# Grid attention in a mixer kernel: the order of scores, scaling, transposes and values of sixteen pairs

## Chip, cores and metric

The kernel runs on one core of one Trainium2 chip. The metric is the device time of one execution in microseconds. The engines are PE (matmuls and transposes; PEld is its weight load), ACT, DVE, POOL and SP, which issues the DMAs. Each works through its instructions in the order in which the program gives them.

## The reference

One layer of a hybrid backbone for 512 latent tokens and 256 context tokens of width 1024, all in float32. A normalised input goes through one wide projection. Its columns feed three mixers: a short gated convolution, a gated linear recurrence in both directions, and attention on the latent grid of 8 rows by 64 columns. The three are gated, merged and projected, and a mixture of 16 experts follows. The change concerns the attention:

```
s_loc = einsum(q, k of the window) * scale + bias     # 256 keys of the grid
s_ctx = einsum(q, k of the context) * scale           # 256 keys of the context
p     = softmax(concat(s_loc, s_ctx))                 # 512 scores a query
o     = einsum(p_loc, v) + einsum(p_ctx, v_ctx)
```

Each of 8 heads has 64 channels. The queries are taken in blocks of 16 columns by 8 rows, 128 queries to a block.

## The kernel before

**Pairs.** The attention is cut into 16 pairs n: two heads that lie together on the 128 partitions (`hp`, four of them) by one block of 128 queries (`cb`, four of them). Four functions make the work of a pair, and each issues at once all that it does on every engine.

- `att_scores(n)`, lines 883 to 902: four matmuls on PE write the scores of both heads into two banks of tag hg (two buffers). Then for each head u in turn: DVE adds the bias (line 897) and takes the row maximum (898), ACT computes the exponential and its row sum into a tile p (900).
- `att_scale(n)`, 904 to 910: for each head DVE takes the reciprocal of the sum (908) and multiplies p by it (909).
- `att_turn(n, u)`, 912 to 922: four PE transposes of p (917) into the bank tp, which has one buffer, and a copy by ACT into a tile pT (919).
- `att_values(n)`, 924 to 942: sixteen matmuls of the values with pT (934) into a bank of tag acc; after every fourth pair ACT and DVE (939, 940) split the result into a rounded and a remaining part.

**Foreground.** While this runs, PE also works through eight items of weights: two convolution gates with their products c, u (lines 953 to 968) and b (970 to 975), and two items of raw gates. An item has two blocks of eight steps; a step is three matmuls of 128x512 (line 453). After the eighth step of a block its result is evacuated by ACT (c, gate) or DVE (u, b). `use_item` (424 to 439) also hangs four pieces of the split of the next item's weights on steps 0, 2, 5 and 8: a cast on ACT (366) and a subtraction on DVE (367) that reads the cast. With three leftover steps that turn value rows (862 to 869) the foreground has 131 entries.

**Order.** The order of all instructions is the order of the Python calls. `weave` (180 to 192) lays the list `att_bg` evenly among the foreground entries: after each of these it issues as many entries of the list as are due by the share of the foreground's cost that is done. An entry None issues nothing but takes its place, so it sets distances. Before the change the list has 83 entries, five to a pair.

**Around it.** Before the stage lie the projections and the recurrence; behind it lie the remaining gates and the merge, and then the experts, whose weights are loaded into the tiles that the earlier stages give back.

Of the kernel before, what the change touches and what calls it, by code (L numbers as in the profile page):

```python
# [146 lines left out]
def mixer_moe(ctx: ExitStack, tc: tile.TileContext, a, out):  # L147
# [10 lines left out]
    def bank(tag):  # L158
        return psum.tile([128, 512], F32, tag=tag, name=tag, bufs=pbufs[tag])
# [8 lines left out]
    def g512(dt=F32):  # L168
        return gen.tile([128, 512], dt, tag="g", name="g", bufs=NA_)
# [707 lines left out]
    def att_load(hp):  # L877
        for t in range(3):
            b_ = gen.tile([128, 2, 256], F32, tag="bias", name="bias", bufs=4)
            SP.dma_start(out=b_, in_=a["bias"][2 * hp:2 * hp + 2, :, 256 * t:256 * t + 256].rearrange("u p k -> p u k"))  # L880
            ast["b", hp, t] = b_

    def att_scores(n):
        def f():
            hp, cb = au[n]
            if cb == 3 and hp < 3:
                att_load(hp + 1)
            rs = [slice(64 * u, 64 * u + 64) for u in range(2)]
            ps = [bank("hg") for _ in range(2)]
            qs = nq[hp][:, 128 * cb:128 * cb + 128]  # L890
            for c, keys in enumerate((nk[hp][:, 64 * KB0[cb]:64 * KB0[cb] + 256],
                                      nkc[hp // 2][:, 256 * (hp % 2):256 * (hp % 2) + 256])):
                for u in range(2):
                    PE.matmul(ps[u][:, 256 * c:256 * c + 256], qs[rs[u]], keys[rs[u]], start=True, stop=True)
            for u in range(2):
                st_ = gen.tile([128, 4], F32, tag="st", name="st", bufs=4)
                V.tensor_tensor(ps[u][:, 0:256], ps[u][:, 0:256], ast["b", hp, BTYPE[cb]][:, u], op=ALU.add)
                V.tensor_reduce(st_[:, 0:1], ps[u], axis=AX.X, op=ALU.max, negate=True)  # L898
                p = g512()
                S.activation(p, ps[u], AF.Exp, bias=st_[:, 0:1], accum_out=st_[:, 1:2])  # L900
                ast["p", n, u] = (p, st_)
        return f

    def att_scale(n):
        def f():
            for u in range(2):
                p, st_ = ast["p", n, u]
                V.reciprocal(st_[:, 2:3], st_[:, 1:2])
                V.tensor_scalar(p, p, st_[:, 2:3], None, op0=ALU.mult)
        return f  # L910

    def att_turn(n, u):
        def f():
            p, _ = ast["p", n, u]
            pt = bank("tp")
            for c in range(4):
                PE.transpose(pt[:, 128 * c:128 * c + 128], p[:, 128 * c:128 * c + 128], ident)
            pT = g512()
            S.copy(pT, pt)
            ast["t", n, u] = pT  # L920
            del ast["p", n, u]
        return f

    def att_values(n):
        def f():
            hp, cb = au[n]
            pT = [ast.pop(("t", n, u)) for u in range(2)]
            if cb == 0:
                ast["o"] = bank("acc")
            po = ast["o"]  # L930
            vs = (nv["lat"][:, KB0[cb]], nv["lat"][:, KB0[cb] + 2], nv["ctx"][:, 0], nv["ctx"][:, 1])
            for c in range(4):
                for u in range(2):
                    PE.matmul(po[64 * u:64 * u + 64, 128 * cb:128 * cb + 128],
                              vs[c][:, 128 * hp + 64 * u:128 * hp + 64 * u + 64],
                              pT[u][:, 128 * c:128 * c + 128], start=(c == 0), stop=(c == 3))
            if cb == 3:
                hi, lo = g512(F32R), g512(F32R)
                S.copy(nat_q(hi), perm_q(po))
                V.tensor_tensor(nat_q(lo), perm_q(po), nat_q(hi.bitcast(F32)), op=ALU.subtract)  # L940
                yv[2][hp] = (hi, lo)
        return f

    att_bg = [att_scores(0)]
    for n in range(16):
        att_bg += [att_values(n - 1) if n else None, att_scale(n), att_scores(n + 1) if n < 15 else None,
                   att_turn(n, 0), att_turn(n, 1)]
    att_bg += [None, att_values(15)]


    cst = {}
# [172 lines left out]
    for pr in range(2):  # L1124
        for i in (2 * pr, 2 * pr + 1):
            n = 16 + 3 * pr + (i % 2)
            fg += use_item(n, [proj(n, 0, ev_c(i)), proj(n, 1, ev_u(i))])
        n = 18 + 3 * pr
# [367 lines left out]
```

## Time and profile before

| | us |
|---|---|
| median of 3 runs | 1749.94 |
| lowest and highest run | 1746.86, 1750.92 |
| profiled execution, its own time | 1747.9 |
| its span in the profile | 1745.7 |
| PE busy | 1633.8 (94%) |
| DVE busy | 570.7 (33%) |
| ACT busy | 369.2 (21%) |

The profile is of one execution. The span lies between its first and last instruction. A busy PE is not a PE at its peak, because matmuls overlap; the granted clock says at which share of full speed the throttle let it run. The stage of the change lies from about 392 to 562 us.

### The profile page before, as it was taken

Reading aid. Unit: us, or ns where it says so; the run is one execution under the profiler, and the core shown is the slowest. Engines: PE = TensorE matmul, PEld = TensorE weight load, DVE = VectorE, ACT = ScalarE, POOL = GpSimd, SP = SyncE. Lnnn points to the kernel's source line nnn. Section 1 sums busy time; section 2 is a strip of 40 time slices with the busy share of each in tenths; the row PEclk is TensorE's granted clock in tenths of the full one; section 3 lists DMA queues with packets and bytes.
Section 4 is the critical chain, followed back from the end, with each engine's and each line's share of the span. In section 5 each row is a group of like instructions: output and inputs, shape, how many; then the busy total and the mean of one; then the engine's idle time right before and its main releaser. Section 6 shows DMA issues by size and latency. Waiting matters only on the chain.

```text
span 1745.7 us, 20467 instructions
## 1 busy us (share of the span) xinstructions
PE 1633.8 (94%) x8382; PEld 928.4 (53%) x8382; DVE 570.7 (33%) x1135; ACT 369.2 (21%) x759; POOL 79.9 (5%) x150
## 2 busy tenths in 40 slices
PE   4999999998989999999999999999998998989988
PEld 2767888775666888896343343343432432424322
DVE  2518776445654343334012111121121121201121
ACT  3514445333434232323000000000000100000000
POOL 0314330000000000000000000000000000000000
PEclk8999999999999999999999999999999999999999
DMA  8870111111111332356999999999999999999997
GB/s 342 268 256 25 49 49 73 49 67 67 67 61 43 109 137 102 144 221 240 411 426 427 426 426 427 426 427 426 427 426 427 427 426 427 426 426 427 427 426 293
DMA packets 80745, 487.77 MB, mean 279 GB/s; under 512 B 8972, under 2 KB 12556, under 8 KB 25740
## 3 DMA queue, kind: packets, MB, share of 16 engines
q1 hardware_dynamic: 80652, 486.47, 68.2%
q8 instruction: 66, 1.08, 0.2%
q14 instruction: 27, 0.22, 0.0%
HBM read 484.34 MB, written 2.10 MB: 279 GB/s over the span
## 4 chain that ended last, share of the span: by engine, by line
PE 62%; DMA 18%; DVE 8%; ACT 2%; issue 1%; ACTq 0%; SPq 0%; DVEq 0%
PE pj L1365 17%; PE pj L453 17%; PE acc L1390 7%; DMA B<-in_w_exp_dram 7%; DMA W<-in_w_exp_dram 6%; PE pj L1016 4%; PE hg L1419 4%; PE hg L1333 3%; PE pj L1197 2%; DMA C<-in_w_exp_dram 2%; DMA A<-in_w_exp_dram 2%; DVE st L898 1%; DVE acc L1422 1%; DMA D<-in_w_exp_dram 1%; PE hg L724 1%
## 5 line engine op out<-in xcount | busy, mean ns | idle before, releaser
L453 PE MATMUL pj<-A,W 128*128 128x512 f32 x1536 | 410.8, 406 | 2.9 <-ACT W L366 1.9
L453 PEld LDWEIGHTS pj<-A,W 128*128 128x128 f32 x1536 | 275.6, 190 | 73.1 <-issue 21.4
L367 DVE TENSOR_TENSOR W<-W 128x512 fp32r<-128x512 f32 (+1 forms) x184 | 122.0, 686 | 167.0 <-ACT W L366 166.7
L1372 DVE TENSOR_TENSOR s<-s,pj 128x512 f32<-128x512 f32 x32 | 22.0, 687 | 444.4 <-PE pj L1365 357.7
L1365 PE MATMUL pj<-W,xe 128*64 128x512 f32 x688 | 155.1, 598 | 4.1 <-DMA W<-in_w_exp_dram 4.1
L1370 ACT ACTIVATE s<-pj 128x512 f32<-128x512 f32 x32 | 19.1, 597 | 556.6 <-PE pj L1365 556.6
L1365 PE MATMUL pj<-A,xe 128*64 128x512 f32 x512 | 116.8, 600 | 3.7 <-DMA A<-in_w_exp_dram 3.7
L1419 PE MATMUL hg<-ye,oht 64*128 64x512 f32 x240 | 100.6, 685 | 16.6 <-DVE acc L1422 16.6
L1365 PEld LDWEIGHTS pj<-W,xe 128*64 128x64 f32 x688 | 47.9, 137 | 104.8 <-issue 91.3
L366 ACT CAST W<-W 128x512 fp32r<-128x512 f32 (+1 forms) x184 | 103.3, 600 | 0.0
L1365 PE MATMUL pj<-B,xe 128*64 128x512 f32 x432 | 98.2, 596 | 5.1 <-DMA B<-in_w_exp_dram 5.1
L1422 DVE TENSOR_TENSOR acc<-acc,hg 128x512 f32<-128x512 f32 x120 | 77.7, 685 | 37.3 <-PE hg L1419 37.3
L1365 PEld LDWEIGHTS pj<-A,xe 128*64 128x64 f32 x512 | 35.1, 138 | 78.3 <-issue 65.4
L1419 PEld LDWEIGHTS hg<-ye,oht 64*128 64x128 f32 x240 | 32.8, 194 | 81.8 <-DVE acc L1422 69.6
L1411 DVE TENSOR_TENSOR ye<-mod,acc 64x512 f32<-64x512 f32 x30 | 20.6, 686 | 170.0 <-PE acc L1390 169.5
L1390 PE MATMUL acc<-W,at 128*64 128x512 f32 x320 | 71.5, 595 | 1.3 <-DMA W<-in_w_exp_dram 1.3
L1365 PEld LDWEIGHTS pj<-B,xe 128*64 128x64 f32 x432 | 29.7, 137 | 67.9 <-issue 54.0
L1380 ACT COPY at<-tp 128x512 f32<-128x512 f32 x32 | 18.7, 586 | 216.6 <-PE tp L1378 216.1
L453 PEld LDWEIGHTS pj<-C,W 128*128 128x128 f32 x384 | 59.2, 190 | 9.2 <-ACT y L625 0.8
L453 PE MATMUL pj<-C,W 128*128 128x256 f32 x384 | 61.7, 283 | 0.0
L1365 PE MATMUL pj<-C,xe 128*64 128x512 f32 x256 | 59.1, 603 | 1.0 <-DMA C<-in_w_exp_dram 1.0
L1333 PEld LDWEIGHTS hg<-ot,xn 128*128 128x128 f32 x512 | 57.9, 192 | 2.7 <-issue 2.7
(287 smaller groups left out, 1813.0 us busy)
## 6 DMA issues: line engine op xcount, KB each, us to landing
W<-in_w_exp_dram SPq DMA_DIRECT2D x126, 1024.0 KB, 19.5
A<-in_w_exp_dram SPq DMA_DIRECT2D x88, 1024.0 KB, 19.6
B<-in_w_exp_dram SPq DMA_DIRECT2D x85, 1024.0 KB, 19.5
C<-in_w_exp_dram SPq DMA_DIRECT2D x42, 1024.0 KB, 19.6
D<-in_w_exp_dram SPq DMA_DIRECT2D x42, 1024.0 KB, 19.6
W<-in_w_in_dram SPq DMA_DIRECT2D x34, 1024.0 KB, 4.8
y<-in_w_mod_dram SPq DMA_DIRECT2D x32, 256.0 KB, 6.0
g<-in_w_mod_dram SPq DMA_DIRECT2D x32, 256.0 KB, 5.2
```

The lines of the kernel that those rows point to most:

```text
L366: S.copy(hi[:, sl], raws[n][:, sl])
L367: V.tensor_tensor(lo[:, sl], raws[n][:, sl], hi[:, sl].bitcast(F32), op=ALU.subtract)
L453: PE.matmul(dst, w[wi][:, k, 128 * b:128 * b + 128], src[xi][:, k], start=(k == 0 and p == 0), stop=(k == KT - 1 and p == 2))
L1016: PE.matmul(st["p"], wb[wi][:, 4 * br + k], yv[br][k][xi], start=(k == 0 and p == 0), stop=(k == 3 and p == 2))
L1197: PE.matmul(st["p"][:, 256 * u:256 * u + 256], mm[k][mi][:, ts], w[wi][:, k], start=(k == 0 and p == 0), stop=(k == KT - 1 and p == 2))
L1333: PE.matmul(px[:, 128 * k:128 * k + 128], xn[:, i, 128 * kk:128 * kk + 128], ot[:, 128 * i:128 * i + 128], start=(i == 0), stop=(i == 3))
L1365: PE.matmul(pg[64 * u:64 * u + 64], xp[:, kk, 64 * (e % 2):64 * (e % 2) + 64], wt[:, k, 512 * u:512 * u + 512], start=(kk == 0), stop=(kk ...
L1372: V.tensor_tensor(est["s", j], est["s", j], pg, op=ALU.mult)
L1390: PE.matmul(est["y"][64 * u:64 * u + 64], lhs, wt[:, k, 512 * u:512 * u + 512], start=(kk == 0), stop=(kk == 15))
L1411: V.tensor_tensor(ye[us], mod5[us, 512 * u:512 * u + 512], y[us], op=ALU.mult)
L1419: PE.matmul(pc, oht[64 * u:64 * u + 64, 128 * i:128 * i + 128], ye[64 * u:64 * u + 64], start=True, stop=True)
L1422: V.tensor_tensor(av, av, pc, op=ALU.add)
```

## The change

The scores of pair 0 come first as before. Then each pair n has its two turns with the values of pair n-1 between them, then the scores of pair n+1, two empty entries, and the scaling of pair n+1. The functions themselves are the same. The list grows to 115 entries, seven to a pair.

```diff
-    att_bg = [att_scores(0)]
+    att_bg = [att_scores(0), None, None, None, att_scale(0)]
     for n in range(16):
-        att_bg += [att_values(n - 1) if n else None, att_scale(n), att_scores(n + 1) if n < 15 else None,
-                   att_turn(n, 0), att_turn(n, 1)]
-    att_bg += [None, att_values(15)]
+        att_bg += [att_turn(n, 0), att_values(n - 1) if n else None, att_turn(n, 1)]
+        att_bg += [att_scores(n + 1), None, None, att_scale(n + 1)] if n < 15 else [None, att_values(15)]
```

## Rows read from the trace of the kernel before

**Rows 1.** Stages by windows; columns: us, PE, PEld, DVE, ACT, POOL, clock, DMA, GB/s.
```profile
392.00:562.00 170.00, 150.04 (x904) 108.00 (x903) 89.97 (x187) 67.71 (x145) 0.00 (x0) 0.98 0.18 61
562.00:780.00 218.00, 217.78 (x1123) 185.78 (x1121) 86.98 (x142) 67.84 (x142) 10.29 (x8) 1.00 0.37 138
780.00:1745.00 965.00, 908.28 (x4218) 350.87 (x4218) 181.27 (x344) 75.28 (x139) 0.18 (x1) 0.99 0.98 410
```

**Rows 2.** Groups by line and shape, 388 to 565 us: busy, mean ns, idle before.
```profile
L917 PE MATMUL tp<-ident,g 128*128 128x128 f32 x128 | 20.1, 279 | 17.8 <-ACT g L919 16.3 <-ACT nvc L869 1.5
```

**Rows 3.** Timeline, scores of pair 4: start, us, engine, line [idle before <-releaser].
```profile
431.22 1.14 PE L894 MATMUL hg<-g 64*128 64x256 f32 x8
...
432.28 1.66 PE L453 MATMUL pj<-A,W 128*128 128x512 f32 x6
432.38 0.43 DVE L897 TENSOR_TENSOR hg<-hg,bias 128x256 f32<-128x256 f32 x1 [2.00 <-PE hg L894]
...
433.77 0.60 PE L917 MATMUL tp<-ident,g 128*128 128x128 f32 x4
433.91 0.69 DVE L898 TENSOR_REDUCE st<-hg 128x1 f32<-128x512 f32 x1
...
434.70 0.69 ACT L900 ACTIVATE g<-hg,st 128x512 f32<-128x512 f32 x1 [0.28 <-DVE st L898]
435.28 0.19 ACT L900 ACTIVATION_READ_ACCUMULATOR g<-hg,st 128x1 f32 x1
435.38 0.57 ACT L919 COPY g<-tp 128x512 f32<-128x512 f32 x1
...
436.00 0.66 PE L917 MATMUL tp<-ident,g 128*128 128x128 f32 x4 [0.93 <-ACT g L919]
...
436.70 0.59 ACT L919 COPY g<-tp 128x512 f32<-128x512 f32 x1 [0.75 <-PE tp L917]
...
438.99 2.33 PE L453 MATMUL pj<-A,W 128*128 128x512 f32 x9
```

**Rows 4.** Timeline, an unbroken run of projection matmuls in the merge stage.
```profile
599.68 11.27 PE L453 MATMUL pj<-A,W 128*128 128x512 f32 x49
```

**Rows 5.** Timeline, pieces of the weight split, a reciprocal and a scaling.
```profile
424.77 0.60 ACT L366 CAST W<-W 128x512 fp32r<-128x512 f32 x1
...
425.41 0.69 DVE L367 TENSOR_TENSOR W<-W 128x512 fp32r<-128x512 f32 x1 [1.41 <-ACT W L366]
...
524.24 0.68 DVE L367 TENSOR_TENSOR W<-W 128x512 fp32r<-128x512 f32 x1
524.84 0.15 DVE L908 RECIPROCAL st<-st 128x1 f32<-128x1 f32 x1
...
525.03 0.49 DVE L909 TENSOR_SCALAR g<-g,st 128x512 f32<-128x512 f32 x1
```

**Rows 6.** Timeline, evacuations of the products u and b on DVE, and what follows.
```profile
416.69 0.69 DVE L962 TENSOR_TENSOR g<-g,pj 128x512 f32<-128x512 f32 x1 [2.81 <-PE pj L453]
...
419.39 1.28 DVE L367 TENSOR_TENSOR W<-W 128x512 fp32r<-128x512 f32 x2
...
448.09 0.69 DVE L973 TENSOR_TENSOR g<-g,pj 128x512 f32<-128x512 f32 x1 [0.20 <-PE pj L453]
...
450.07 0.68 DVE L367 TENSOR_TENSOR W<-W 128x512 fp32r<-128x512 f32 x1
```

**Rows 7.** Windows and timeline around two gaps on PE, and the granted clock.
```profile
482.00:492.00 10.00, 7.78 (x43) 5.66 (x42) 4.79 (x10) 4.24 (x9) 0.00 (x0) 0.83 0.01 2
502.00:512.00 10.00, 8.33 (x50) 5.99 (x50) 7.02 (x14) 3.13 (x7) 0.00 (x0) 1.00 0.04 7
...
487.09 0.66 PE L917 MATMUL tp<-ident,g 128*128 128x128 f32 x4 [2.22 <-ACT g L919]
...
491.64 2.33 PE L453 MATMUL pj<-A,W 128*128 128x512 f32 x9
...
509.48 0.66 PE L917 MATMUL tp<-ident,g 128*128 128x128 f32 x4 [1.67 <-ACT g L919]
```

## The prediction

> **What bounds the kernel now.** I first cut the span into stages [rows 1]. From 562 us on there is nothing that could absorb a delay: from 562 to 780 PE is busy 217.78 of 218 us, and from 780 to the end the DMA engines carry 410 GB/s at a share of 0.98, fed by loads that start only when the merge stage gives its tiles back. A microsecond lost or won before 562 us is one microsecond of the end. The change sits in the first of the three windows, 392 to 562 us, where PE is busy 150.04 of 170 us. The grouped view by line says who makes it idle there [rows 2]: 17.8 us before the transposes (line 917), 16.3 of them released by the copy on ACT (line 919) and 1.5 once by an earlier copy. I call these the present gaps.
>
> One period of the timeline shows how a gap arises [rows 3]. The scores of pair 4 start on PE at 431.22. The second of their two exponentials runs on ACT from 434.70, with its sum read out until 435.47 (435.28 + 0.19). The copy of the first transposes of pair 3 stands behind them in ACT's order and starts at 435.38; the second transposes write the same single bank (tp) and start at 436.00, after a gap of 0.93 us. The gap is thus a matter of the order on ACT: the scores of n+1 go between the two turns of n.
>
> **Part 1, what is removed.** With both turns ahead of the scores, ACT has only the odd weight cast in front of a copy, and the values of pair n-1 and two or three projection steps stand on PE between the turns; transposes, two steps and the values take 2.99 us (436.00 to 438.99). With ACT free the copy starts 0.70 us behind the start of the transposes (436.00 to 436.70) and runs 0.59. So the 17.8 us go, all of them. If that cover failed, they would stay (a rival below).
>
> **Part 2, what is late next.** The list of background entries grows from 83 to 115 (empty ones counted) over the same 131 foreground entries, so one entry now comes every 131/115 = 1.14 steps, not every 1.58. Before, six entries (9.5 steps) lie between the scores of a pair and its first transposes; now four do: 4.56 steps, in the integer rule of `weave` five for pairs 1 to 7 and 15, four for pairs 8 to 14. A step is three matmuls; 49 of them take 11.27 us [rows 4], so 0.23 each and 0.69 a step. The scores hold PE 1.06 us (431.22 to 432.28 [rows 3]); some 0.1 goes at the switch (432.28 to 433.77 is 1.49 for two steps). PE arrives at the first transposes 4.6 us (five steps) or 3.9 us (four) after the start of the scores.
>
> Is the scaled row there by then? The chain, from the start of the scores [rows 3]: first bias add at 1.16, second maximum at 2.69 (433.91), second exponential at 3.48 (434.70), ACT free for its next instruction at 4.16 (435.38). With nothing between, DVE would do the first reciprocal at 3.3, and the scaling, 0.19 later and 0.49 long [rows 5], would end at 4.0. That just fits.
>
> But something is between. Each item of 16 steps carries four pieces of the weight split, after steps 0, 2, 5 and 8: a cast on ACT (line 366) and a subtraction on DVE (line 367) that waits for it. Eight steps make a period, so the pieces keep their place: every pair from 1 on has one or two of them between its scores and its scaling. The cast stands on ACT behind both exponentials: 4.16. The subtraction starts 0.64 later (424.77 to 425.41 [rows 5]): 4.80. The reciprocal stands behind it on DVE, 0.60 after its start (524.24 to 524.84): 5.40. The scaling runs from 5.59 to 6.08, and PE can transpose at 6.1. One piece makes PE wait 1.5 us at five steps and 2.2 at four. A second piece adds its 0.60. Where the convolution's product u is evacuated just ahead of the scores, DVE is busy with it for 2.70 us (416.69 to 419.39 [rows 6]). The matmuls that it waits for end about where the scores begin; I let it start 0.2 after them, an estimate, so that the bias add comes at 2.9, 1.7 late. Where the product b is, it is 1.98 us (448.09 to 450.07), so 1.0 late.
>
> Pair by pair, in the order that the code gives: pairs 1, 3, 7 one piece, 1.5 each; 9 and 13 one piece at four steps, 2.2 each; 14 two pieces at four steps, 2.8; 5 and 11 one piece behind b, 2.5 and 3.2; 6 and 12 two pieces behind b, 3.1 and 3.8; 2 and 4 two pieces behind u, 3.8 each; 8 and 10 the same at four steps, 4.5 each; 15 one piece and a gate copy on ACT, 2.0; pair 0 some 0.8 behind the copies of the value rows. The sum is 43.7 us; as the profile counts idle time (about 0.1 less each, since ends are modelled), 42.1.
>
> Behind the waiting transposes on PE are all projection steps, so the wait is the stage's. Behind the waiting reciprocal on DVE are evacuations and subtractions with room: the pj bank has three buffers, and a piece is needed only in the next item, at least seven steps (4.8 us) on. SP's weight loads go out an item ahead and the bias loads keep their place with the scores; POOL has nothing here. These I put at nothing; at worst the pieces of step 8 come late when waits of 4 us pile up, and the cover of 4.8 us is larger. The tail, values 15 two steps behind the last turn and not three, is also nothing: the copy needs 1.3 us.
>
> So PE's idle time goes from 17.8 to 42.1 us: plus 24.3. Bounds: the bare chain without the pieces in its way would leave 9 us (below), so minus 9; if every pair had two pieces behind u at four steps, 16 x 4.4 = 70, so plus 52. I stay at the pairs' own sum, as each term is a row.
>
> **Part 3, the clock.** In the window 482 to 492 the granted clock is 0.83 of full: PE had stood still for 2.22 us before 487.09, and then the clock went to its lower level (1.2 GHz) for some 3.4 us (0.17 x 10 us x 2) [rows 7]. From that start to the first projection step behind the values at 491.64 it took 4.55 us (transposes, two steps, values); the same sequence without a fall takes 2.99 (436.00 to 438.99 [rows 3]). A fall costs 1.56 us. The gap of 1.67 us before 509.48 had none: 502 to 512 shows 1.00. The new gaps: nine of 2.4 us or more, three of 1.9 to 2.1, four of at most 1.4. I take falls behind the nine and half of the three, 10.5, less the one that goes: 9.5 x 1.56 = 14.8 us. Bounds: none at all (0), and twice the price where the gap is long (30).
>
> **Sum.** The profiled execution took 1747.9 us (span 1745.7 and 2.2 around it). 1747.9 + 24.3 + 14.8 = 1787.0. The median of the runs shown, 1749.94, is 2.0 above that execution, in a scatter of 4; I add half and say 1788. The forecast's own range is 1776 to 1802.
>
> **Rivals.**
> (a) The waits come, the clock stays: 1747.9 + 24.3 = 1772. For it: the gap of 1.67 us without a fall. Against: the gap of 2.22 us had one, and nine would be longer.
> (b) The other side: the pieces of the split don't hold up the scaling. Then the scaled row is there at 4.0, or 1.7 and 1.0 later behind u and b; PE waits 1.1 us in pairs 2 and 4, 1.8 in 8 and 10, 0.4 in 5 and 6, 1.1 in 11 and 12, 0.1 in three others: 9 us. 17.8 - 9 and one fall of 1.6 less: 1737. It decides where the subtraction starts before the second exponential ends. For it: the cast needs nothing of the pair. Against: in the rows the copy and the cast stand on ACT in the order of the code, and DVE waited 1.41 us for a cast before 425.41 [rows 5].
> (c) The gap at the second turn stays, because the one bank makes it and not ACT's order: 17.8 and the fall stay on top of the forecast, 1806. Against it: of the 1.61 us from the first transposes' start (433.77) to their copy, all but 0.7 is the two exponentials. The Trainium skill (Perfetto Trace Analysis, section Optimization Strategy) says that a gap which keeps repeating on the engine that should be full can mean that memory for the next tile ran out; by that rule the single tp bank is the cause and the time is 1806. The start of the copy speaks against it, with no run yet that has one bank and a free ACT throughout.
>
> **How the numbers follow.** Forecast 0.62, (a) 0.17, (b) 0.10, (c) 0.08, and 0.03 for losses and gains that cancel. The likeliest is 1788. The range 1766 to 1806 takes in (a) and (c) and leaves out (b) and the tails. Under 0.2% (3.5 us) this kernel's runs can't tell a change from none. Faster 0.10 is (b); within 0.2% is the 0.03; slower 0.87 is the rest.
>
> **What would show it.** Right: in the profile after, line 917's idle time is put down to the scaling on DVE (line 909) and is near 42 us, with the copy on ACT all but gone from the waits on PE; the longest are pairs 8 and 10 (over 4 us); the scores to scores period is 11 to 13 us; eight or more spells of the lower clock lie between 392 and 600 us. Wrong: line 917 waits under 20 us in total, or for ACT still, or the later stages change their length.

## The result and the profile after

The changed kernel takes 1790.54 us (median of 4 runs, 1789.29 to 1791.35); the kernel before takes 1749.29 us (4 runs, 1746.86 to 1750.92). The ratio is 1.0235, with a 95% interval of 1.0223 to 1.0248: 41 us slower. The forecast was 1788, in a range of 1766 to 1806.

The stages by windows, with the columns of [rows 1]:

```profile
388.00:600.00 212.00, 168.10 (x912) 122.13 (x912) 91.71 (x189) 69.58 (x146) 0.00 (x0) 0.90 0.14 49
600.00:820.00 220.00, 219.78 (x1145) 187.48 (x1140) 87.63 (x143) 68.71 (x143) 10.31 (x8) 1.00 0.37 138
820.00:1785.00 965.00, 912.40 (x4213) 353.68 (x4212) 180.87 (x343) 75.34 (x139) 0.18 (x1) 0.98 0.97 410
```

The stage is longer, and in it PE stands still for 44 us and the granted clock is 0.90 of full. The stages behind it look as before. From the first scores to the first matmul of the merge the stage took 169.2 us before (392.19 to 561.42); now it takes 208.9 (391.78 to 600.71): 39.7 of the 41.5 us by which the span grew. The rest lies behind the stage, where the profiles of all the kernels here scatter by 7 us (from the merge to the end 1183.7 to 1190.7 us, in no order with the change). The ends of the stage, in the kernel before and then in the changed one:

```profile
392.19 1.14 PE L894 MATMUL hg<-g 64*128 64x256 f32 x8
...
561.42 5.74 PE L1016 MATMUL pj<-y,W 128*128 128x512 f32 x24
```

```profile
391.78 1.14 PE L894 MATMUL hg<-g 64*128 64x256 f32 x8
...
600.71 5.78 PE L1015 MATMUL pj<-y,W 128*128 128x512 f32 x24
```

The grouped view by line, to be read beside [rows 2]:

```profile
L917 PE MATMUL tp<-ident,g 128*128 128x128 f32 x128 | 22.3, 303 | 41.8 <-DVE st L908 41.3 <-DVE g L909 0.5
```

PE's idle time before the transposes went from 17.8 to 41.8 us, and its releaser from ACT to DVE. Here is one period of the timeline, as in [rows 3]: the scores of pair 3, one piece of the split, its scaling and its first transposes.

```profile
430.08 1.13 PE L894 MATMUL hg<-g 64*128 64x256 f32 x8
...
431.15 3.73 PE L453 MATMUL pj<-A,W 128*128 128x512 f32 x15
431.25 0.43 DVE L897 TENSOR_TENSOR hg<-hg,bias 128x256 f32<-128x256 f32 x1 [4.50 <-PE hg L894]
...
433.59 0.69 ACT L900 ACTIVATE g<-hg,st 128x512 f32<-128x512 f32 x1 [0.29 <-DVE st L898]
434.17 0.19 ACT L900 ACTIVATION_READ_ACCUMULATOR g<-hg,st 128x1 f32 x1
434.27 0.61 ACT L366 CAST W<-W 128x512 fp32r<-128x512 f32 x1
434.91 0.69 DVE L367 TENSOR_TENSOR W<-W 128x512 fp32r<-128x512 f32 x1 [1.44 <-ACT W L366]
435.52 0.16 DVE L908 RECIPROCAL st<-st 128x1 f32<-128x1 f32 x1
...
435.71 0.49 DVE L909 TENSOR_SCALAR g<-g,st 128x512 f32<-128x512 f32 x1
436.11 0.15 DVE L908 RECIPROCAL st<-st 128x1 f32<-128x1 f32 x1
...
436.31 0.42 PEld L917 LDWEIGHTS tp<-ident,g 128*128 128x128 f32 x4 [1.85 <-issue]
436.34 0.63 PE L917 MATMUL tp<-ident,g 128*128 128x128 f32 x4 [1.46 <-DVE st L908]
```

PE has five steps (15 matmuls) between the scores and the transposes, and stands still for 1.46 us behind them. ACT runs the cast straight behind the second exponential; DVE waits 1.44 us for that cast with the reciprocal queued behind. The name of the releaser needs a second look: the transposes read the scaled row (line 909), which ends at 436.20, 0.11 us before PE's weight load at 436.31; the reciprocal of the other head, which they do not read, ends at 436.26, between the two. The view, which infers releasers, names that one, line 908; by the code it is line 909.

A long gap and what the clock does behind it, in the changed kernel (a fall is the clock's step to its lower level, a spell the time that it stays there); first the timeline of pair 2, behind the product u, with the values (line 934) at the lower clock:

```profile
424.19 0.63 PE L917 MATMUL tp<-ident,g 128*128 128x128 f32 x4 [3.69 <-DVE st L908]
...
425.45 1.07 PE L934 MATMUL acc<-g,nvl 128*64 128x128 f32 x8
...
427.30 1.65 PE L453 MATMUL pj<-A,W 128*128 128x512 f32 x3
```

In pair 3 the same eight matmuls of the values and the same step take 0.66 and 0.96 us, at the full clock:

```profile
437.60 0.66 PE L934 MATMUL acc<-g,nvl 128*64 128x128 f32 x8
...
438.62 0.96 PE L453 MATMUL pj<-A,W 128*128 128x512 f32 x3
```

The windows over this period and the next say it in the column of the clock:

```profile
420.00:432.00 12.00, 8.31 (x48) 5.85 (x47) 4.51 (x10) 4.63 (x10) 0.00 (x0) 0.86 0.08 22
432.00:444.00 12.00, 10.54 (x64) 7.77 (x63) 6.35 (x14) 3.24 (x7) 0.00 (x0) 1.00 0.25 87
```

The first holds the gap of 3.69 us and a spell of some 3.4 us (0.14 x 12 us x 2) at the lower level (1.2 GHz); the second holds a gap of 1.46 and none.

### The profile page after: what moved, and what is told of

The parts are those of the page before. It is cut to its first block, busy times and chain, and to the rows that moved or that the text cites. A ratio compares the mean times of both kernels' runs of the same rounds, so it can differ in the third digit from the quotient of the medians.

```text
span 1787.2 us, 20475 instructions
## 1 busy us (share of the span) xinstructions
PE 1653.4 (93%) x8382; PEld 943.3 (53%) x8382; DVE 571.7 (32%) x1135; ACT 370.9 (21%) x759; POOL 79.2 (4%) x150
## 4 chain that ended last, share of the span: by engine, by line
PE 67%; DMA 12%; DVE 9%; ACT 2%; issue 1%; ACTq 0%; DVEq 0%; SPq 0%
PE pj L1364 19%; PE pj L453 16%; PE acc L1389 8%; DMA B<-in_w_exp_dram 5%; PE hg L1418 4%; PE pj L1015 4%; DMA D<-in_w_exp_dram 3%; PE hg L1332 3%; PE pj L1196 2%; DMA W<-in_w_exp_dram 2%; DVE acc L1421 1%; PE acc L934 1%; DVE st L898 1%; DVE W L367 1%; PE tp L917 1%; DMA C<-in_w_exp_dram 1%
## 5 line engine op out<-in xcount | busy, mean ns | idle before, releaser
L453 PE MATMUL pj<-A,W 128*128 128x512 f32 x1536 | 419.6, 413 | 2.9 <-ACT W L366 1.9
L453 PEld LDWEIGHTS pj<-A,W 128*128 128x128 f32 x1536 | 281.1, 194 | 75.4 <-issue 22.8
L917 PE MATMUL tp<-ident,g 128*128 128x128 f32 x128 | 22.3, 303 | 41.8 <-DVE st L908 41.3
```

The lines of the kernel that those rows point to most:

```text
L453: PE.matmul(dst, w[wi][:, k, 128 * b:128 * b + 128], src[xi][:, k], start=(k == 0 and p == 0), stop=(k == KT - 1 and p == 2))
```

## The experiments

Two theories of the wait stood against each other: the pieces of the weight split hold the scaling up on DVE (mine), or the chain of scores, maximum and exponential is itself too long for four or five steps. And two of the time: waits and clock falls as two terms, or waits alone. Times are medians of 4 runs, beside the kernel before on the same chip.

**The scaling in the scores' own entry.**

```diff
-    att_bg = [att_scores(0), None, None, None, att_scale(0)]
+    att_bg = [att_scores_scale(0), None, None, None, None]
...
-        att_bg += [att_scores(n + 1), None, None, att_scale(n + 1)] if n < 15 else [None, att_values(15)]
+        att_bg += [att_scores_scale(n + 1), None, None, None] if n < 15 else [None, att_values(15)]
```

> The changed order, but the scaling of a pair stands directly behind its scores, in the same entry, so that no piece of the weight split is between them on DVE. Theory (the pieces hold the scaling up): the bare chain is left, line 917 idles some 10 us in all, at most 2 us at a time and only behind the products u and b, and the clock falls once (behind the value rows); 1749 - 12 = 1737 us, faster than before. Rival (the chain of scores, maximum and exponential is itself too long for four or five steps): line 917 idles over 30 us and the time stays above 1775.

Measured: 1738.85 us, a ratio of 0.9946 to before (0.9931 to 0.9961). All that PE waits for in the stage, by the view of waits (us in total, times, longest):

```profile
PE tp L917 <- DVE g L909: 7.6, 8, 1.7
PE tp L862 <- ACT nvl L864: 2.1, 1, 2.1
PE tp L917 <- ACT nvc L869: 0.5, 1, 0.5
```

Eight waits are left, those behind the products. The timeline of pair 2, the same as above in the changed kernel, shows why the order on DVE is the cause:

```profile
418.34 0.15 DVE L908 RECIPROCAL st<-st 128x1 f32<-128x1 f32 x1
418.53 0.49 DVE L909 TENSOR_SCALAR g<-g,st 128x512 f32<-128x512 f32 x1
...
419.17 0.63 PE L917 MATMUL tp<-ident,g 128*128 128x128 f32 x4 [0.98 <-DVE g L909]
419.22 1.13 ACT L366 CAST W<-W 128x512 fp32r<-128x512 f32 x2
...
419.96 2.12 DVE L367 TENSOR_TENSOR W<-W 128x512 fp32r<-128x512 f32 x3
```

The scaling now runs before the casts, the gap is 0.98 us and not 3.69, and no clock fall follows. The chain itself does fit, but for what the products leave; the second theory falls.

**The pieces moved behind the scaling.**

```diff
-        at = {int(p * len(flat) / 6): p for p in range(4)}
+        at = {5: 0, 6: 1, 13: 2, 14: 3} if late else {int(p * len(flat) / 6): p for p in range(4)}
```

> The changed order, but in the eight items of this stage the four pieces of the split hang on steps 5, 6, 13 and 14, behind the scaling and not ahead of it. Theory: the same 10 us of idle time at line 917 as with the scaling moved, and 1737 us. Rival (the long chain): above 1775. If only the cast's place on ACT counted and not the subtraction on DVE, this run would gain and the one with the scaling moved would not.

Measured: 1735.01 us, 0.9923 (0.9908 to 0.9938); line 917 waits for line 909 for 7.6 us, as above. The same cause taken away from the other side has the same effect.

**The subtraction on POOL.**

```diff
-                V.tensor_tensor(lo[:, sl], raws[n][:, sl], hi[:, sl].bitcast(F32), op=ALU.subtract)
+                (G if 17 <= n <= 24 else V).tensor_tensor(lo[:, sl], raws[n][:, sl], hi[:, sl].bitcast(F32), op=ALU.subtract)
```

> The changed order; only the subtraction of the weight split of these eight items runs on POOL and not on DVE, the cast stays on ACT where it was. Theory (the scaling stands behind the subtraction in DVE's order): as with the scaling moved, line 917 idles some 8 us and the time is 1739 us, or up to 1745 if POOL slows DVE. Rival (ACT's order with the cast is what holds the scaling): line 917 idles over 30 us and the time stays near 1790.

Measured: 1735.58 us, 0.9927 (0.9911 to 0.9944), again 7.6 us of waits. The cast keeps its place on ACT and every instruction keeps its place in the code; only DVE's queue is rid of the subtraction. So ACT's order alone does not hold the scaling: the in-order queue of DVE does, by an instruction that waits. The timeline of that kernel shows POOL taking 1.29 us for a piece that DVE does in 0.69, beside nothing that waits for it in this stage:

```profile
425.35 0.61 ACT L366 CAST W<-W 128x512 fp32r<-128x512 f32 x1
...
426.03 1.29 POOL L367 TENSOR_TENSOR W<-W 128x512 fp32r<-128x512 f32 x1 [4.68 <-ACT W L366]
```

**The gaps filled with matmuls.**

```diff
+FILL = (0, 6, 15, 6, 16, 10, 12, 6, 18, 9, 18, 12, 15, 8, 10, 7)
...
             pt = bank("tp")
+            if u == 0:
+                for _ in range(FILL[n]):
+                    PE.matmul(pt, hT[0][:, 0, 0:128], hT[0][:, 0], start=True, stop=True)
```

> The changed order, with 6 to 18 matmuls of 128x512 ahead of each pair's first transposes, as many as fit into the gap measured there; their result is overwritten. Theory of two terms (waits 24 us, clock falls some 15 us): PE works through the gaps, the waits stay as work, the falls behind them go (one left, behind the value rows), and the time is 1790 - 15 = 1775 us. Rival (the falls cost nothing, since PE waits for the scaling anyway): 1790 us with a granted clock near 0.985. A third way, the waits being longer than the trace shows: slower than 1790.

Measured: 1771.08 us, 1.013 (1.0108 to 1.0152). The order is that of the change and the transposes come when the scaling lets them; only PE doesn't stand still. The stage takes 190.0 us (392.30 to 582.25) and not 208.9, and the one spell of the lower clock left in it is that behind the value rows near 398 us. The changed kernel has ten more. The window over the stage, to be read beside the first of the three windows of the result (0.90), and the view of waits of this kernel (line 921 is the transposes here, 910 the scaling):

```profile
388.00:590.00 202.00, 197.52 (x1127) 147.67 (x1126) 95.41 (x195) 76.09 (x156) 0.00 (x0) 0.99 0.15 51
```

```profile
PE tp L863 <- ACT nvl L865: 2.1, 1, 2.1
PE tp L921 <- DVE g L910: 1.7, 8, 0.3
PE tp L921 <- ACT nvc L870: 0.5, 1, 0.5
```

So the 41 us are some 23 us of lateness (1.013 of 1748.3) and some 18 us of clock (1.0235 less 1.013; with both intervals 14 to 23). By the lengths of the stage it is 20.8 us (190.0 less 169.2) and 18.9 (208.9 less 190.0). The third way, waits longer than the trace shows, did not come.

**A second bank for the second turn, in the order of before.**

```diff
-            pt = bank("tp")
+            pt = bank("pj" if u else "tp")
```

> The order of before, but the second turn of a pair writes a bank of tag pj (three buffers, of which the projections of this stage use two at a time) and not the single tp bank. If order on ACT and the single bank make the gap only together, a second bank alone removes it: line 917 idles under 3 us, the fall of the clock near 487 us goes, 1748 - 18 = 1730 us. If the copy's place behind the exponentials held up more than the bank, the values would wait instead and the time would stay within 5 us of 1748.

Measured: 1733.63 us, 0.9915 (0.99 to 0.9929), and the fall near 487 us is gone. Part of the wait moved on: the values now wait for the late copies, 3.6 us in 8 gaps, and the transposes once.

```profile
PE acc L934 <- ACT g L919: 3.6, 8, 0.6
PE tp L862 <- ACT nvl L864: 2.1, 1, 2.1
PE tp L917 <- ACT nvc L869: 1.7, 1, 1.7
```

The gap of before thus needed both, the single bank and the exponentials ahead of the copy, and either remedy takes it away: in the changed kernel, with one bank, no second transposes wait for line 919.

**Scores two pairs ahead.**

```diff
-    att_bg = [att_scores(0), None, None, None, att_scale(0)]
+    att_bg = [att_scores(0), None, None, att_scores(1), None, att_scale(0)]
     for n in range(16):
         att_bg += [att_turn(n, 0), att_values(n - 1) if n else None, att_turn(n, 1)]
-        att_bg += [att_scores(n + 1), None, None, att_scale(n + 1)] if n < 15 else [None, att_values(15)]
+        att_bg += [att_scale(n + 1) if n < 15 else None, att_scores(n + 2) if n < 14 else None]
+    att_bg += [att_values(15)]
```

> Both turns ahead of the scores as in the change, but the scores run two pairs ahead, so that a whole period lies between the scores and the scaling: turn, values of n-1, turn, scaling of n+1, scores of n+2. Theory: the gap of before and that of after both go, line 917 idles 3 to 5 us, one or two falls of the clock, 1749 - 16 = 1733 us. Rival (one tp bank is what makes the gap before the second transposes): line 917 waits for line 919 again by some 15 us, and the time is 1745 to 1750.

Measured: 1729.76 us, 0.9902 (0.9887 to 0.9917). The turns stand ahead of the scores, as in the change, and a whole period now lies between the scores and the scaling. Line 917 idles 3.0 us, and the one fall left in the stage is that near 398 us:

```profile
PE tp L862 <- ACT nvl L864: 2.1, 1, 2.1
PE tp L917 <- ACT g L919: 1.8, 3, 0.8
PE tp L917 <- DVE st L908: 1.2, 1, 1.2
```

**The same with the pieces moved and the first scores behind the value rows.**

```diff
-    att_bg = [att_scores(0), None, None, att_scores(1), None, att_scale(0)]
+    att_bg = [None] * 4 + [att_scores(0), None, att_scores(1), None, att_scale(0)]
```

> Scores two pairs ahead, the pieces of the split on steps 5, 6, 13 and 14, and the first scores behind the turned value rows. Theory: the fall of the clock near 398 us goes as well with the gap of 2.1 us there, line 917 idles some 3 to 4 us, and the stage from the first scores to the merge is 143 us where two pairs ahead alone had 150.4: 1723 us. Rival: the front of the stage only moves the gap to the first pair, and the time stays at 1730.

Measured: 1729.2 us, 0.9888 (0.9874 to 0.9903), which can't be told from the run without (the intervals overlap). The fall near 398 us and the wait behind the value rows are gone, and from the first scores to the merge it is 143.2 us, as expected. But the expectation took the whole difference of 7 us in that length as gain, while the first scores now start at 396.73 and not 391.75: 5 of the 7 us are the mark that moved. The merge starts at 539.96 and not 542.13, 2.2 us earlier, which the scatter behind the stage covers.

## Why the prediction was right

**The direction and the mechanism.** The steps held in their order. Line 917 idles 41.8 us where 42.1 was forecast, and waits on line 919 are gone from PE. Pair by pair the gaps were, from 0 to 15: 0.46, 1.44, 3.69, 1.46, 3.97, 2.37, 3.00, 1.49, 4.37, 2.15, 4.37, 3.07, 3.65, 2.14, 2.41, 1.70 us, twelve of them within 0.1 of the forecast's wait less 0.1. Pairs 8 and 10 are the longest, as said. Pair 4 came out 0.3 longer: its second exponential starts 0.40 us behind the end of its maximum and not 0.12 as in the others, for a reason that the trace does not show. Pairs 0, 14 and 15 came out 0.2 to 0.3 shorter. For 14 and 15 the reason is in the timeline: the pieces there belong to the first merge item and are 384 wide, not 512, so two of them hold DVE 1.03 us and not 1.29. Such rows stood in the trace of before and were overlooked.

**The clock.** Ten gaps drew a fall and one fall of before is gone: nine more, against 9.5 forecast, but not behind quite the same gaps: 2.41 us had none, 2.14 and 2.15 had one each. In the stage 39.7 - 24.0 = 15.7 us are not idle time, where 14.8 was forecast. Two of the spells, near 398 and 527 us, lasted 6.8 us and not 3.4, which the forecast had not; counted in spells of 3.4 us there are eleven more than before, at 1.4 us each where 1.56 was the price. The run with the gaps filled has twelve fewer than the changed kernel and a stage shorter by 18.9 us, 1.6 each. It gives the share of the clock directly, 14 to 23 us, and puts an end to rival (a), which had the waits without the clock.

**Rival (b)**, the pieces not holding the scaling up, is not what the change did; but its arithmetic was that of three runs. They measured 7.6 us of waits behind the products, where 9 was worked out, and 1735 to 1739 us where 1737 was. **Rival (c)**, that the one bank makes the gap, is refuted for this order by the changed kernel itself. The rule of the Trainium skill behind it (Perfetto Trace Analysis, section Optimization Strategy), that a repeating bubble can mean too little memory for the next tile, was a true hint all the same: a second bank removes the gap of before.

**What was wrong.** The releaser was to be line 909; the view names line 908, for the reason given with the timeline. And the time from the end of the scaling to the transposes was put at nearly nothing, while it is 0.11 us; over 16 pairs that is under 2 us. One sign named ahead did not come: the period from scores to scores was to be 11 to 13 us and ran from 10.6 to 16.2, 13.1 in the mean. The sum had the same waits and falls in it, so the forecast of the time does not suffer; the sign was put too narrow for gaps of 1.4 to 4.4 us with a fall behind most of them.

**Nothing behind the stage took part.** The loss of 39.7 us in the stage came out as 41 at the end; within their scatter of 7 us the merge and the experts hid none of it.

## What to carry to other kernels

When a softmax is moved closer to its consumer, count the steps that are left, and walk the chain through each engine's queue with everything that the code issues in between: one instruction that waits (here a subtraction for its cast) delays all that stands behind it on that engine, though it has nothing to do with them. Put the link that the bottleneck waits for ahead of the work with slack, or lengthen the distance by a whole period: scores two pairs ahead took 0.990 of the time before where the change took 1.0235. And price a new gap on PE twice, as its length and as what the clock does behind it; here the second was two thirds to nine tenths of the first (15.7 beside 24.0 us by the idle time, 18.9 beside 20.8 by the gaps filled).

## What the runs showed of the hardware

In the changed kernel gaps on PE of 2.14 and 2.15 us were followed by the lower clock and one of 2.41 us was not. Pairs 13 and 14, each with the window behind its gap (columns of [rows 1]):

```profile
570.81 0.63 PE L917 MATMUL tp<-ident,g 128*128 128x128 f32 x4 [2.14 <-DVE st L908]
583.87 0.63 PE L917 MATMUL tp<-ident,g 128*128 128x128 f32 x4 [2.41 <-DVE st L908]
570.00:578.00 8.00, 7.19 (x42) 5.51 (x44) 1.18 (x5) 1.68 (x3) 0.00 (x0) 0.79 0.35 133
583.00:591.00 8.00, 7.13 (x49) 5.29 (x50) 3.39 (x10) 1.96 (x4) 0.00 (x0) 1.00 0.00 0
```

At line 917 the gaps of 1.44 to 1.70 us in the changed kernel had no fall, and all of 3.00 us or more had one. But with the pieces moved behind the scaling, a gap of 1.62 us at the value rows, with one of 0.46 us close behind it, was followed by a fall too:

```profile
396.51 0.55 PE L862 MATMUL tp<-ident,g 128*128 128x128 f32 x3 [1.62 <-ACT nvl L864]
396.00:404.00 8.00, 7.02 (x33) 5.25 (x33) 2.97 (x7) 3.63 (x7) 0.00 (x0) 0.79 0.00 1
```

So between 1.6 and 2.4 us the outcome can't be told from the length of the gap alone; what else decides it, no run here shows. Most spells lasted 3.4 us; two lasted twice as long.

POOL could take the subtractions (1.29 us each and not 0.69) with no loss that the time shows. Of the 32 scalings on DVE 14 ran in part beside one of them and kept their 0.49 us; no reciprocal ran beside one, so that for those nothing is shown.
